# Making the low parts of 16 projection weights on VectorE instead of GpSimd, in a two-layer decoder step

## The chip, the cores and the metric

The kernel runs on one core of a Trainium2 chip. The metric is device time in microseconds for one execution of the whole program: the median of the runs shown, lower is better. A core has TensorE (PE in the profile), VectorE (DVE), ScalarE (ACT), GpSimd (POOL) and SyncE (SP), which here only issues transfers.

## The reference

One inference step of a decoder trunk with two layers, for a prompt of 1024 tokens and 8 samples of 8 tokens (1088 columns in all), with D = 1024. Cut to what matters:

```python
# layer 0
y, ... = mix_ab(hp, ...)      # y = concatenate([a_out, b_out], -1) @ w_out   (w_out 1024 x 1024)
xp = xp + y
# layer 1
yp, kp, vp = swa_prompt(...)  # y = o.reshape(N, T, N_HEADS * HEAD_DIM) @ w_o   (w_o 1024 x 1024)
ys, ks_, vs_ = swa_sample(...)
xp, xs = xp + yp, xs + ys
# each layer, after that
xp = xp + mem_attend(rmsnorm(xp, ln_mem[l]), mk, mv, m_w_q[l], m_q_gain[l], m_w_o[l])
xp = xp + conv_ffn(rmsnorm(xp, ln_ffn[l]), ...)
```

The two output projections are `@ w_out` in layer 0 and `@ w_o` in layer 1. All of it is float32.

## The kernel before

**Precision.** TensorE multiplies operands of type fp32r, and each product of the large projections is made of three: a value is split into a high part (a copy to fp32r) and a low part (the value minus its high part), and `mm3` (lines 259 to 261) adds high times high, high times low and low times high into one PSUM tile. So every weight and every activation tile needs two instructions before TensorE can use it: an ACTIVATE on ScalarE for the high part, and a subtraction for the low part. For a weight, `split_w` (lines 228 to 235) makes both for a tile of 128 partitions x 1024 elements: line 233 the high part, line 234 the low part. Line 234 runs on the engine that its argument names, `(eng or P)`, so on GpSimd if none is given. For an activation, `split_act` makes both, on ScalarE (line 360) and VectorE (line 361).

**The output projections.** `out_proj` (line 603) is called once in each layer. It goes through pairs (g, c): g is one of four groups of 256 output rows, c one of three chunks of the 1088 columns (384, 384 and 320). For a group it calls the loader twice, which gives two weights of 128 x 1024. Then, for each of eight blocks k of the inputs, it splits the activation tile (lines 360 and 361) and issues six matmuls, three for each of the two weights. After k = 7 `x_update` adds the two results into the residual stream: VectorE reads PSUM (line 313), GpSimd adds the old low part (line 314), ScalarE and VectorE split the sum again (292, 293), and ScalarE with GpSimd or VectorE sums its squares (300 to 305). The loader of layer 0 is `load_cols`, that of layer 1 is `load_wo`, inside `swa`. Each makes eight weights in a run, 16 in all.

**Around them.** In layer 0 the projection follows the values of the gating block: `v_tile` for nine tiles t (lines 539 to 547, with a step on GpSimd at 547), and `gate(t)`, four matmuls (line 559), a sum on VectorE (562 or 564) and a product on GpSimd (568). `gate(7)` and `gate(8)` stand in the middle of the projection, behind step 11. In layer 1 the attention of the samples runs in steps between those of the projection (`next(smp)`): scores, a softmax over the keys (lines 1673 to 1688, with eight exponentials on ScalarE at 1683), transposes, values (1718, 1719).

**Order and buffers.** The order on TensorE is that of the code. The order on every other engine is made by a scheduler at build time, which models the durations; each engine then runs its row strictly in that order. A load lands in one of three staging tiles `st`, which comes free when the low part has been made. The weights' parts live in ten tiles `w`, two for each weight.

Of the kernel before, what the change touches and what calls it, by code (L numbers as in the profile page):

```python
# [71 lines left out]
def kernel(  # L72
# [10 lines left out]
    V, S, P, T = nc.vector, nc.scalar, nc.gpsimd, nc.tensor  # L83
    mm = T.matmul

    def pool(name, bufs=1, **kw):
        return tc.tile_pool(name=name, bufs=bufs, reuse_waits="tile", **kw)
# [7 lines left out]
    def f(ap):  # L95
        return ap.bitcast(F32)

    def psA():
        return pa.tile([128, 512], F32, tag="a", name="psa")
# [39 lines left out]
    def stage():  # L139
        return wp.tile([128, 1024], F32, tag="st", name="st", bufs=3)  # L140
# [4 lines left out]
    def wtile():  # L145
        return Pair(wslot(), wslot())
# [81 lines left out]
    def split_w(st, shape, gain, eng=None):  # L228
        if gain is not None:
            v = st.rearrange("p (k m) -> p k m", k=shape[0])  # L230
            (eng or P).tensor_tensor(out=v, in0=v, in1=gain.unsqueeze(2).to_broadcast([128, shape[0], shape[1]]), op=ALU.mult)
        w = wtile()
        S.activation(w[:, 0, :], st, AF.Copy)
        (eng or P).tensor_tensor(out=w[:, 1, :], in0=st, in1=f(w[:, 0, :]), op=ALU.subtract)
        return w

    def load_cols(src, c0, gain=None, k=KB, eng=None):
        st = stage()
        m = 1024 // k
        nc.sync.dma_start(out=st.rearrange("p (k m) -> p k m", k=k),  # L240
                          in_=src[:, c0:c0 + m].rearrange("(k p) m -> p k m", p=128))
        w = split_w(st, (k, m), gain, eng)
        return w.rearrange("p s (k m) -> p s k m", k=k)
# [14 lines left out]
    def mm3(out, ah, al, bh, bl, first, last):  # L258
        mm(out, lhsT=ah, rhs=bh, start=first, stop=False)  # L259
        mm(out, lhsT=ah, rhs=bl, start=False, stop=False)  # L260
        mm(out, lhsT=al, rhs=bh, start=False, stop=last)  # L261
# [48 lines left out]
    def x_update(c, m, ps):  # L310
        n = CHS[c][1]
        t1 = tmp()[:, :n]
        V.tensor_tensor(out=t1, in0=ps[:, :n], in1=f(xh[c][:, m, :]), op=ALU.add)
        P.tensor_tensor(out=t1, in0=t1, in1=f(xl[c][:, m, :]), op=ALU.add)
        if c == 2:
            nc.sync.dma_start(out=xd[:, m, :], in_=t1)
        split_x(c, m, t1)
# [40 lines left out]
    def split_act(pl, src_n, src, tag="s3"):  # L358
        t = pl.tile([128, 2, 384], F32R, tag=tag, name=tag)
        S.activation(t[:, 0, :src_n], src, AF.Copy)  # L360
        V.tensor_tensor(out=t[:, 1, :src_n], in0=src, in1=f(t[:, 0, :src_n]), op=ALU.subtract)  # L361
        return t
# [48 lines left out]
    def mix0(sst):  # L411
        w_in = ab_w_in[0]
        with ExitStack() as es:
# [138 lines left out]
            def gate(t):  # L552
                c, o, w = tile_of(t)
                vt = vts.pop(t)
                ps = psB()
                pv = ps.rearrange("p (g i) -> p g i", g=4)[:, :, :w]
                for g in range(4):
                    rhs = wst[:, g, :] if t < 8 else bd[:, g, :]
                    mm(pv[:, g, :], lhsT=vt[:w, 128 * g:128 * g + 128], rhs=rhs, start=True, stop=True)
                sg = bp.tile([128, 4, 128], F32, tag="sg", name="sg", bufs=1)  # L560
                if t < 8:
                    V.tensor_tensor(out=sg, in0=pv, in1=bsb, op=ALU.add)
                else:
                    V.tensor_tensor(out=sg[:, :, :64].rearrange("p g (n t) -> p g n t", t=8),
                                    in0=pv.rearrange("p g (n t) -> p g n t", t=8),
                                    in1=bsb[:, :, 0:8].unsqueeze(2).to_broadcast([128, 4, 8, 8]), op=ALU.add)
                uv = u32[:, :, 128 * t:128 * t + w]
                P.tensor_tensor(out=uv, in0=uv, in1=sg[:, :, :w], op=ALU.mult)
# [15 lines left out]
            for t in range(NT):  # L584
# [3 lines left out]
                if t == 3:  # L588
                    pool_states()
                    e2.close()  # L590
                    sp = es.enter_context(pool("m0o", 9))
# [2 lines left out]
                if t == 5:  # L594
                    conv_ctx(0)
            src = lambda k, c: (u32 if k < 4 else b32)[:, k % 4, CHS[c][0]:CHS[c][0] + CHS[c][1]]
            for i, _ in enumerate(out_proj(src, lambda m: load_cols(ab_w_out[0], 128 * m), sp,
                                           [(g, c) for g in range(4) for c in range(3)])):
                if i == 11:
                    gate(7)  # L600
                    gate(8)

    def out_proj(src, loader, sp, order):
        ws = {}
        for g, c in order:
            if g not in ws:
                ws[g] = [loader(2 * g), loader(2 * g + 1)]
            n = CHS[c][1]
            pss = [psA(), psA()]
            for k in range(KB):  # L610
                s3 = split_act(sp, n, src(k, c))
                for i in range(2):
                    w = ws[g][i]
                    mm3(pss[i][:, :n], w[:, 0, k, :], w[:, 1, k, :], s3[:, 0, :n], s3[:, 1, :n], k == 0, k == KB - 1)
                if k == KB - 1:
                    for i in range(2):
                        x_update(c, 2 * g + i, pss[i])
                yield g, c, k
# [844 lines left out]
    def swa(wkv):  # L1463
        sc = 64.0 ** -0.5
        with ExitStack() as es:
            bp = es.enter_context(pool("swa"))
            qo = bp.tile([128, 8, 1088], F32, name="qo")
            if True:
# [260 lines left out]
                def load_wo(m):  # L1729
                    st = stage()  # L1730
                    sv = st.rearrange("p (g j m) -> p g j m", g=2, j=4)
                    src = c_w_o[0][:, 128 * m:128 * m + 128].rearrange("(g w j d) m -> w g d j m", g=2, w=2, j=4)
                    for w in range(2):
                        for g in range(2):
                            nc.sync.dma_start(out=sv[64 * w:64 * w + 64, g], in_=src[w, g])
                    wt = split_w(st, None, None)
                    return wt.rearrange("p s (k m) -> p s k m", k=KB)

                for t in range(NT):
# [32 lines left out]
                sp = es.enter_context(pool("swao", 5))  # L1772
                src = lambda k, c: qo[:, k, CHS[c][0]:CHS[c][0] + CHS[c][1]]
                order = [(0, 0), (0, 1), (1, 0), (1, 1), (0, 2), (1, 2), (2, 0), (2, 1), (2, 2), (3, 0), (3, 1), (3, 2)]
                for i, (g, c, k) in enumerate(out_proj(src, load_wo, sp, order)):
                    if i % 4 == 2:
                        next(smp, None)
                    if i == 31:
                        for _ in smp:
                            pass  # L1780

    with tc.manual_schedule(engines={mybir.EngineType.PE}):
        with ExitStack() as rs:
            with ExitStack() as es:
                open_tmp(es, 0)
                mix0(mem_kv())
                kept = mem(0, rs)
            x32, conv_out = ffn(0, *kept, rs)
            with ExitStack() as es:
                open_tmp(es, 1)  # L1790
                wkv = [load_rows(c_w_qkv[0], r, 1024, g_mix[1][:, 2 * r:2 * r + 2]) for r in range(4)]
                after_ffn(0, x32, conv_out)
                rs.close()
                swa(wkv)
                kept = mem(1, rs)
            x32, conv_out = ffn(1, *kept, rs)
            final(x32, conv_out)
# [28 lines left out]
```

## Time and profile before

| | |
|---|---|
| median of 3 runs | 2620.58 us (2615.94 to 2621.81) |
| the profiled execution, its own time | 2620.95 us |
| its span, first to last instruction | 2619.2 us |
| mean granted clock of TensorE | 0.970 |
| busy: TensorE, VectorE, ScalarE, GpSimd | 95%, 75%, 47%, 17% |

The 1.75 us between the span and the profiled execution's time lie around the program. A busy share is a mean over the whole span: VectorE is nearly always busy in some stages and half idle in others. A granted clock of 1.00 is 2.4 GHz and 0.50 is 1.2 GHz; a value between them is a mean over a stretch with both.

### The profile page before, as it was taken

The page shows a single profiled execution, that of the slowest core. Times are in us where ns is not written, and L with a number is a line of the kernel's source. Part 1 is how long each engine was busy: PE and PEld are TensorE (multiplying, and loading weights), DVE is VectorE, ACT ScalarE, POOL GpSimd, SP SyncE. Part 2 cuts the span into 40 slices and gives each one's busy share as a digit, 9 for nine tenths or more (in the row PEclk, how much of TensorE's full clock was granted, in tenths as well). Part 3 has the DMA queues.
Part 4 walks back from the last instruction along what each step waited for, and adds up shares of the span by engine and source line. Part 5 has one row for each costly group of instructions (what it writes and reads, how often), then busy time and mean ns, then how long its engine had stood idle before and what let it go on. Part 6 is the DMA issues. An engine that isn't in the chain of part 4 may idle for free.

```text
span 2619.2 us, 46210 instructions
## 1 busy us (share of the span) xinstructions
PE 2489.4 (95%) x17136; PEld 2305.6 (88%) x17136; DVE 1969.7 (75%) x4551; ACT 1232.5 (47%) x2705; POOL 456.7 (17%) x434
## 2 busy tenths in 40 slices
PE   8999999779999999999999989998699999999998
PEld 7998988679999998999876768877599999999998
DVE  7646965787878786888767676856988787777885
ACT  7324645354554544333555564553454545455331
POOL 2516532110000001110133333421100000002100
PEclk9999999889999999999999987999799999999999
DMA  8302112523333346654211011205424343348642
GB/s 278 118 12 71 64 38 93 178 83 124 116 124 124 105 129 211 220 194 141 68 39 48 1 58 49 77 26 160 140 92 135 96 130 107 120 148 294 228 143 86
DMA packets 229345, 305.53 MB, mean 117 GB/s; under 512 B 17793, under 2 KB 189919, under 8 KB 229118
## 3 DMA queue, kind: packets, MB, share of 16 engines
q1 hardware_dynamic: 213502, 227.91, 27.3%
q0 software_dynamic: 15616, 74.65, 7.9%
q8 instruction: 135, 2.21, 0.4%
q14 instruction: 92, 0.75, 0.1%
HBM read 217.79 MB, written 84.63 MB: 115 GB/s over the span
## 4 chain that ended last, share of the span: by engine, by line
issue 31%; PE 30%; DVE 11%; DMA 4%; ACT 3%; POOL 1%; SPq 0%; ACTq 0%; DVEq 0%; POOLq 0%
PE psa L1021 3%; PE psa L1022 3%; PE psa L1023 3%; PE psa L259 3%; PE psa L260 3%; PE psa L261 3%; PE psb L1021 2%; PE psb L1023 2%; PE psb L1022 2%; DMA st<-in_f_w_down_dram 2%; DVE s L361 1%; PE psb L167 1%; DVE w L1070 1%; DVE x L1393 1%; PE psa L1622 1%
## 5 line engine op out<-in xcount | busy, mean ns | idle before, releaser
L1069 ACT ACTIVATE w<-st 128x512 fp32r<-128x512 f32 (+2 forms) x532 | 299.0, 572 | 381.1 <-PE psb L1023 103.8
L1070 DVE TENSOR_TENSOR w<-st,w 128x512 fp32r<-128x512 f32 (+2 forms) x532 | 325.8, 617 | 180.4 <-ACT w L1069 171.3
L1021 PE MATMUL psa<-b,w 128*128 128x272 f32 x1152 | 334.4, 290 | 20.5 <-ACT b L1105 12.5
L1022 PE MATMUL psa<-b,w 128*128 128x272 f32 x1152 | 332.7, 289 | 9.0 <-DVE b L1106 9.0
L1023 PE MATMUL psa<-b,w 128*128 128x272 f32 x1152 | 333.3, 289 | 0.0
L1021 PE MATMUL psa<-big,w 128*128 128x272 f32 x960 | 280.7, 292 | 8.0 <-ACT x L1391 4.0
L1023 PE MATMUL psa<-big,w 128*128 128x272 f32 x960 | 280.2, 292 | 1.5 <-DVE w L1070 1.5
L1022 PE MATMUL psa<-big,w 128*128 128x272 f32 x960 | 278.9, 290 | 0.0
L1021 PE MATMUL psb<-big,w 128*128 128x272 f32 x888 | 257.4, 290 | 0.7 <-ACT x L1391 0.4
L1023 PE MATMUL psb<-big,w 128*128 128x272 f32 x888 | 257.3, 290 | 0.0
L1022 PE MATMUL psb<-big,w 128*128 128x272 f32 x888 | 256.5, 289 | 0.0
L1021 PEld LDWEIGHTS psa<-b,w 128*128 128x128 f32 x1152 | 217.4, 189 | 22.6 <-ACT b L1105 13.1
L1022 PEld LDWEIGHTS psa<-b,w 128*128 128x128 f32 x1152 | 217.3, 189 | 11.4 <-DVE b L1106 11.4
L1023 PEld LDWEIGHTS psa<-b,w 128*128 128x128 f32 x1152 | 217.2, 189 | 0.0
L260 PE MATMUL psa<-s,w 128*128 128x384 f32 (+1 forms) x576 | 199.5, 346 | 13.8 <-DVE s L361 13.5
L259 PE MATMUL psa<-s,w 128*128 128x384 f32 (+1 forms) x576 | 199.9, 347 | 2.6 <-ACT s L360 2.6
L1021 PE MATMUL psb<-b,w 128*128 128x272 f32 x696 | 201.6, 290 | 0.0
L1022 PE MATMUL psb<-b,w 128*128 128x272 f32 x696 | 200.4, 288 | 1.2 <-DVE b L1377 1.2
L1023 PE MATMUL psb<-b,w 128*128 128x272 f32 x696 | 201.5, 289 | 0.0
L261 PE MATMUL psa<-s,w 128*128 128x384 f32 (+1 forms) x576 | 196.1, 340 | 0.0
L1021 PEld LDWEIGHTS psa<-big,w 128*128 128x128 f32 x960 | 182.8, 190 | 10.7 <-DVE x L1393 5.8
L1023 PEld LDWEIGHTS psa<-big,w 128*128 128x128 f32 x960 | 183.5, 191 | 1.9 <-DVE w L1070 1.9
(367 smaller groups left out, 6585.1 us busy)
## 6 DMA issues: line engine op xcount, KB each, us to landing
st<-in_f_w_up_dram SPq DMA_DIRECT2D x88, 512.0 KB
hd<-big SPq DMA_DIRECT2D x264, 136.0 KB
hd<-m SPq DMA_DIRECT2D x176, 136.0 KB
big<-hd POOLq DMA_DIRECT2D x48, 408.0 KB, 7.2
st<-in_f_w_down_dram SPq DMA_DIRECT2D x48, 384.0 KB
b<-hd POOLq DMA_DIRECT2D x18, 816.0 KB, 7.3
big<-hd POOLq DMA_DIRECT2D x18, 816.0 KB, 7.7
ks<-in_m_w_kv_dram SPq DMA_DIRECT2D x16, 512.0 KB
```

The source lines that it names most:

```text
L167: T.transpose(out, in_, idt[:rows, :rows])
L259: mm(out, lhsT=ah, rhs=bh, start=first, stop=False)
L260: mm(out, lhsT=ah, rhs=bl, start=False, stop=False)
L261: mm(out, lhsT=al, rhs=bh, start=False, stop=last)
L361: V.tensor_tensor(out=t[:, 1, :src_n], in0=src, in1=f(t[:, 0, :src_n]), op=ALU.subtract)
L1021: mm(ps[:, :QT], lhsT=wt[:, 0, k, :], rhs=bt[:, 0, k, :], start=first and k == 0, stop=False, skip_group_check=True)
L1022: mm(ps[:, :QT], lhsT=wt[:, 0, k, :], rhs=bt[:, 1, k, :], start=False, stop=False, skip_group_check=True)
L1023: mm(ps[:, :QT], lhsT=wt[:, 1, k, :], rhs=bt[:, 0, k, :], start=False, stop=k == nk_of(j) - 1, skip_group_check=True)
L1069: S.activation(t[:, 0], src, AF.Copy)
L1070: V.tensor_tensor(out=t[:, 1], in0=src, in1=f(t[:, 0]), op=ALU.subtract)
L1393: V.tensor_tensor(out=x, in0=ps, in1=x, op=ALU.add)
L1622: mm(po[64 * two:64 * two + 64, :], lhsT=vv[:, t + 1 - nb + kb, 64 * (2 * g + two):64 * (2 * g + two) + 64], rhs=pTs[two, kb], start=(kb = ...
```

## The change

Both loaders now hand VectorE to `split_w`, so that line 234 runs on VectorE for the 16 weights of the two output projections. The other 16 instructions of line 234 stay on GpSimd.

```diff
@@ mix0
-            for i, _ in enumerate(out_proj(src, lambda m: load_cols(ab_w_out[0], 128 * m), sp,
+            for i, _ in enumerate(out_proj(src, lambda m: load_cols(ab_w_out[0], 128 * m, eng=V), sp,
                                            [(g, c) for g in range(4) for c in range(3)])):
@@ swa, load_wo
-                    wt = split_w(st, None, None)
+                    wt = split_w(st, None, None, V)
```

What follows is how the build places them. TensorE's row is the same before and after.

On VectorE, in layer 0 around the last two tiles of the gating block. `vt_2123` is tile 7 and `bn_2170` belongs to tile 8; `s3_2292` and `s3_2301` are the first two activation tiles of the chunk (g = 0, c = 1); the `w` tiles are the low parts of weights 2 to 5. The signs are those of the difference, after against before:

```order
 L335 TENSOR_SCALAR s_2130<-mv_2127 128x1
+L234 TENSOR_TENSOR w_2198<-st_2195,w_2197 128x1024
 L546 TENSOR_SCALAR vt_2123<-vt_2123,mv_2127,s_2129 128x512
+L234 TENSOR_TENSOR w_2489<-st_2486,w_2488 128x1024
 L361 TENSOR_TENSOR s3_2292<-u32_742,s3_2292 128x384
+L234 TENSOR_TENSOR w_2495<-st_2492,w_2494 128x1024
 L541 BN_STATS bn_2170<-vt_2168 64x6
 L562 TENSOR_TENSOR sg_2186<-psb_2181,bsb_746 128x512
+L234 TENSOR_TENSOR w_2773<-st_2770,w_2772 128x1024
 L543 BN_AGGR mv_2172<-bn_2170 64x2
-L335 TENSOR_SCALAR s_2175<-mv_2172 64x1
 L361 TENSOR_TENSOR s3_2301<-u32_742,s3_2301 128x384
```

Four low parts now stand ahead of the last steps of tile 8, and of the tiles of chunk 1.

On VectorE, in layer 1, early in the projection. `s3_17285`, `s3_17294` and `s3_17303` are the activation tiles k = 0, 1 and 2 of (g = 0, c = 1), the next ones that TensorE needs there; 1678 to 1688 are the softmax of the samples; `psa_17174` and `psa_17175` are the results of (0, 0):

```order
 L361 TENSOR_TENSOR s3_17259<-qo_14310,s3_17259 128x384
+L361 TENSOR_TENSOR s3_17285<-qo_14310,s3_17285 128x384
 L1678 TENSOR_TENSOR s_17207<-s_17205,snks_91 128x8
+L361 TENSOR_TENSOR s3_17294<-qo_14310,s3_17294 128x384
+L313 TENSOR_TENSOR t_17268<-psa_17174,big_72 128x384
+L313 TENSOR_TENSOR t_17275<-psa_17175,big_72 128x384
 L1684 TENSOR_TENSOR s_17210<-s_17210,s_17207 128x8
 L1686 RECIPROCAL s_17220<-s_17210 128x8
-L313 TENSOR_TENSOR t_17268<-psa_17174,big_72 128x384
+L361 TENSOR_TENSOR s3_17303<-qo_14310,s3_17303 128x384
 L1688 TENSOR_TENSOR k4_17080<-k4_17080,s_17220 128x1088
-L361 TENSOR_TENSOR s3_17285<-qo_14310,s3_17285 128x384
```

The three activation tiles, which stood behind 1684 to 1688, now stand ahead of 1688, two of them ahead of 1684. ScalarE's row moves with them: the high parts of the first two now stand ahead of the eight exponentials instead of behind.

On VectorE, in layer 1, where the third group begins. `s3_17814` and `s3_17823` are activation tiles of (1, 2), and the two `w` tiles are weights 6 and 7:

```order
 L313 TENSOR_TENSOR t_17767<-psa_17686,big_72 128x320
+L234 TENSOR_TENSOR w_17883<-st_17877,w_17882 128x1024
 L361 TENSOR_TENSOR s3_17814<-qo_14310,s3_17814 128x320
+L234 TENSOR_TENSOR w_18164<-st_18158,w_18163 128x1024
 L361 TENSOR_TENSOR s3_17823<-qo_14310,s3_17823 128x320
 L293 TENSOR_TENSOR big_72<-t_17759,big_72 128x320
```

Two low parts now stand between activation tiles of the chunk in work.

## Rows read from the trace of the kernel before

**Rows 1.** The page: busy time, share of the span and instructions of each engine.

```profile
PE 2489.4 (95%) x17136; PEld 2305.6 (88%) x17136; DVE 1969.7 (75%) x4551; ACT 1232.5 (47%) x2705; POOL 456.7 (17%) x434
```

**Rows 2.** Waits of TensorE: who for whom, us in total, times, longest.

```profile
PE psa L260 <- DVE s L361: 13.5, 15, 2.5
...
PE psb L352 <- DVE rvq L305: 8.6, 2, 4.4
```

**Rows 3.** Stretches: length, busy PE, PEld, DVE, ACT, POOL; PE clock, DMA, GB/s.

```profile
244.40:255.00 10.60, 8.20 (x39) 7.51 (x39) 5.48 (x11) 4.43 (x12) 7.67 (x8) 0.84 0.06 15
255.00:292.00 37.00, 36.68 (x224) 35.95 (x223) 36.76 (x57) 25.64 (x57) 18.97 (x14) 1.00 0.11 38
292.00:301.00 9.00, 7.07 (x32) 6.75 (x32) 9.00 (x12) 4.90 (x13) 5.54 (x4) 0.82 0.48 143
...
1553.90:1564.10 10.20, 6.76 (x21) 5.63 (x20) 9.72 (x14) 6.17 (x15) 6.21 (x4) 0.67 0.20 52
...
1622.00:1632.40 10.40, 7.27 (x28) 6.75 (x28) 10.19 (x13) 5.69 (x11) 7.70 (x6) 0.67 0.43 133
```

**Rows 4.** Groups of GpSimd: busy us, mean ns of one, idle before.

```profile
L234 POOL TENSOR_TENSOR w<-st,w 128x1024 fp32r<-128x1024 f32 x32 | 82.1, 2572 | 54.4 <-ACT w L233 53.2 <-DMA st<-in_ab_w_in_dram 1.2
```

**Rows 5.** Groups of VectorE, shapes apart; columns as in the group before.

```profile
L361 DVE TENSOR_TENSOR s<-b,s 128x384 fp32r<-128x384 f32 x32 | 16.9, 560 | 0.0
...
L1597 DVE TENSOR_TENSOR k<-k,s 128x1024 f32<-128x1024 f32 x14 | 17.1, 1225 | 0.2
```

**Rows 6.** GpSimd in order of time: start us, us, idle before and its releaser.

```profile
227.71 4.94 POOL L234 TENSOR_TENSOR w<-st,w 128x1024 fp32r<-128x1024 f32 x2
...
264.46 2.72 POOL L234 TENSOR_TENSOR w<-st,w 128x1024 fp32r<-128x1024 f32 x1
...
1431.36 2.37 POOL L234 TENSOR_TENSOR w<-st,w 128x1024 fp32r<-128x1024 f32 x1 [7.09 <-ACT w L233]
```

**Rows 7.** VectorE in order of time; columns as in the group before.

```profile
227.78 2.62 DVE L546 TENSOR_SCALAR vt<-vt,mv,s 128x512 f32<-128x512 f32 x1 [1.65 <-POOL s L336]
...
234.44 7.28 DVE L361 TENSOR_TENSOR s<-u,s 128x384 fp32r<-128x384 f32 x3
...
264.84 3.90 DVE L361 TENSOR_TENSOR s<-u,s 128x384 fp32r<-128x384 f32 x2
...
293.27 3.76 DVE L255 SCALAR_TENSOR_TENSOR w<-st,vec,w 128x512 fp32r<-128x512 f32 x2
...
1428.28 0.15 DVE L1594 TENSOR_TENSOR s<-s 128x4 f32<-128x4 f32 x1
...
1431.41 2.34 DVE L1594 TENSOR_TENSOR s<-s 128x4 f32<-128x4 f32 x1 [1.51 <-ACT s L1593]
...
1521.86 2.35 DVE L1594 TENSOR_TENSOR s<-s 128x4 f32<-128x4 f32 x1
...
1554.35 0.17 DVE L1684 TENSOR_TENSOR s<-s 128x8 f32<-128x8 f32 x1 [2.87 <-ACT k L1683]
...
1555.09 1.28 DVE L1688 TENSOR_TENSOR k<-k,s 128x1088 f32<-128x1088 f32 x1
```

**Rows 8.** TensorE in order of time; columns as in group 6.

```profile
245.69 1.16 PE L559 MATMUL psb<-bd,vt 64*128 64x64 f32 x8 [1.26 <-POOL vt L547]
...
297.55 0.50 PE L260 MATMUL psa<-s,w 128*128 128x384 f32 x1 [1.93 <-DVE s L361]
...
1436.05 1.09 PE L167 MATMUL psa<-idt,k 128*128 128x128 f32 x8 [2.84 <-POOL k L1597]
...
1557.70 0.69 PE L260 MATMUL psa<-s,w 128*128 128x384 f32 x1 [2.48 <-DVE s L361]
...
1564.03 1.97 PE L167 MATMUL psb<-idt,k 128*128 128x128 f32 x16
...
1626.55 0.64 PE L260 MATMUL psa<-s,w 128*128 128x320 f32 x1 [2.48 <-DVE s L361]
```

**Rows 9.** ScalarE in order of time, layer 0, the fifth weight.

```profile
233.84 1.06 ACT L233 ACTIVATE w<-st 128x1024 fp32r<-128x1024 f32 x1 [1.18 <-DMA st<-in_ab_w_out_dram]
```

## The prediction, made before the changed kernel ran

> **What bounds the kernel now.** I began with the page's engine line: TensorE is busy 95% of the span, GpSimd 17% [rows 1]. So the end is set by TensorE's work and by the few places where it waits or runs at a lower clock; a change off TensorE can win or lose only there. Next I read TensorE's waits, for places that the change can reach. It waits 13.5 us in 15 waits for the activation low parts of line 361, which VectorE makes in the row in which the new work is put, and 8.6 us for rvq of line 305 [rows 2], behind a projection. Then the stretches of the two projections, engine by engine [rows 3]. Read the VectorE column first: 36.76 of 37 us, 9.00 of 9. Where the projection runs, VectorE is full although its mean is 75%. From 255 to 292 TensorE keeps pace all the same (36.68, clock 1.00). In the four other stretches it doesn't:
>
> - 244.4 to 255: idle 10.60 − 8.20 = 2.40, clock 0.84
> - 292 to 301: idle 1.93, clock 0.82
> - 1553.9 to 1564.1: idle 3.44, clock 0.67
> - 1622 to 1632.4: idle 3.13, clock 0.67
>
> A clock under 1.00 is time on the 1.2 GHz level, and the rows show it behind each of these idles. Its cost is at most (1 − clock) times the length: 1.7, 1.6, 3.4 and 3.4 us. Some of that is idle counted again, so I take three quarters of it.
>
> **The price of one line 234.** On GpSimd it is 2.57 us, 32 times [rows 4]. On VectorE there is no such row. The nearest is line 1597, the same shape with two inputs from SBUF: 1.225 us [rows 5]. So VectorE gets 16 x 1.23 = 19.6 us of work. At first sight that is bad, since it is the full engine.
>
> But look at what VectorE does while GpSimd runs line 234. At 1431.41 it starts line 1594, 128 x 4 elements, which took 0.15 us three us before; now 2.34. It ends with GpSimd's instruction, which ran from 1431.36 to 1433.73 [rows 6, 7]. At 227.78, under two of line 234, a line 546 takes 2.62 us; from 234.44 three of line 361 take 7.28 together and from 264.84 two take 3.90 [rows 7], where one is 0.56 [rows 5]. So in these places VectorE already pays about 2.2 us for a low part that GpSimd makes. Making it itself costs 1.23 and takes the 2.2 away: a gain of about 1.0 us of VectorE, not a loss. What may hide here is the reverse: next to GpSimd's remaining line 314 a line 234 on VectorE may be stretched too. I bound it by 1.23 (as line 1597) and 2.57 (as on GpSimd) and take 1.23, since GpSimd loses its longest instruction in these stages.
>
> **Where it reaches TensorE.** Six places, in time.
>
> *244.4 to 255.* TensorE waits 1.26 us at 245.69 for GpSimd's line 547 of tile 8 [rows 8]. That waited for line 546 on VectorE, behind the stretched tiles of [rows 7]. The new row has four low parts ahead of that tile, 4 x 1.23 = 4.9 us; the four instructions that leave GpSimd there blocked VectorE for about 4 x 2.2 = 8.8. So tile 8 comes about 4 us sooner and the wait, the low clock behind it and the later short waits go: 2.40 + 0.75 x 1.7 = 3.7 us. One condition: the fifth weight's high part ran only at 233.84, after a wait for its load [rows 9], since its staging tile came free only with an earlier low part. VectorE's row now stops at that low part if the load is late. As the low parts before it are made sooner, the load is issued sooner on SP's queue, so I cost this at nothing; uncovered, it would cost about the 1.2 us of that wait.
>
> *292 to 301.* One low part on GpSimd stretches two of line 255 to 3.76 us in all [rows 7] and TensorE waits 1.93 for line 361 at 297.55 [rows 8]. With 1.0 us less in the row and a shorter head of it, I take idle and clock: 1.93 + 0.75 x 1.6 = 3.1.
>
> *1431.* TensorE waits 2.84 at 1436.05 for line 1597 on GpSimd [rows 8], whose softmax sum was line 1594, stretched to 2.34. One low part now stands in that row instead: 2.34 − 1.23 = 1.1.
>
> *1521.* The same stretched line 1594, 2.35 [rows 7], and no wait of TensorE that I can tie to it alone: 0.5.
>
> *1553.9 to 1564.1.* Here the order itself changes. Before, VectorE stood 2.87 us idle at line 1684 for the exponentials and then did line 1688, 1.28 us [rows 7], with the next activation tiles behind both; TensorE waited 2.48 at 1557.70 [rows 8]. In the 10.2 us before its transposes at 1564.03 it does only 21 matmuls [rows 3], which at full clock are 3.4 us (36.68 for 224 in the stretch from 255). In the new row these tiles stand ahead of 1688 and two ahead of 1684, so TensorE works through the exponentials. I leave 1.3 us of waits, chosen, since the transposes need the softmax and the exponentials now stand behind two more high parts on ScalarE: 10.2 − 3.4 − 1.3 = 5.5.
>
> *1622 to 1632.4.* TensorE waits 2.48 at 1626.55 for line 361 [rows 8]. Two low parts now stand among the tiles of that chunk, 2 x 1.23, so most of the wait is only exchanged for another. Of 3.13 + 0.75 x 3.4 = 5.7 I take 2.0.
>
> Sum: 3.7 + 3.1 + 1.1 + 0.5 + 5.5 + 2.0 = 15.9. Against the profiled execution, 2620.95, 0.4 over the median: **2605**. The other low parts (227 to 243, 255 to 292, 1538 to 1557) lie where TensorE keeps pace; there the exchange costs nothing as long as VectorE's row gets shorter. GpSimd's line 314, 547 and 568 no longer queue behind 2.6 us, which I count as nothing since VectorE, not GpSimd, is last there. The wait for rvq behind the projections can move either way by the order of a few 0.4-us steps: ±1.5, in the range.
>
> **Rivals.**
> *Only the order counts.* If VectorE needs 2.57 for line 234 beside GpSimd's other work, each exchange is 2.2 for 2.57, and nothing is left but the 5.5 of the fourth stretch: 2615.5. For it: 314 and 305 still run beside it. Against: the sixteen include many with GpSimd otherwise idle.
> *No change.* The waits are given back later: at the edge to the memory attention, where TensorE waits up to 4.4 us for rvq [rows 2], or at the exponentials. About 2621. Against: VectorE's last work before that edge is shortened too.
> *Slower, a full VectorE.* If VectorE loses under a line 234 of GpSimd less than 1.23 us, the exchange is a loss. That is its deciding point. Twelve of the 16 start in a stretch of [rows 3] or under a stretched row of [rows 7] (the other four at 216, 1539, 1548 and 1620); if GpSimd had cost it nothing there, the price would be 12 x 1.23 = 14.8 us: 2636. With half of that hidden, 2628. Against it are the 2.34, 7.28 and 3.90 of [rows 7], all over that point.
> A rule speaks here: the Trainium skill, "Perfetto Trace Analysis", Optimizing Scalar/DVE Operations, says that a saturated VectorE is a reason to hand work to GpSimd, but that the two share a port to SBUF, so that handing over may not help. By its first half this change goes the wrong way and ends near 2636; by its second half GpSimd's share was not free. The stretched rows of VectorE in this trace side with the second half.
>
> **The numbers.** The forecast has a chance of 0.70, order only 0.12, no change 0.10, slower 0.08. The forecast's own range is 2597 to 2613: the lower end is all idle and the whole bound on the clock of the four stretches (10.9 + 10.1 = 21.0) plus the 2.84 at 1436, 23.8 in all; the upper is half of the sum. What a measurement of this kernel can tell from no change is about 0.2%, 5.2 us. Faster by more: 0.70 and half of "order only", 0.76; within: the other half and "no change", 0.16; slower: 0.08. The range for 8 in 10 is 2596 to 2617, with the forecast and "order only", and with 1.5 for rvq.
>
> **What would show it.** In the profile after: line 234 of VectorE 16 times at a mean near 1.23, and of GpSimd 16 times; near 2.5 on VectorE the first rival holds. Line 1594 in layer 1 at 0.15 each time. No wait for line 547 near 245, TensorE's clock 1.00 through the stretches that answer to the first two, the group of transposes after (0, c = 1)'s third block some 5.5 us sooner against the start of that chunk, and the waits for line 361 well under 13.5. The prediction is wrong if VectorE stops at low parts whose load or high part is late, if the wait for line 361 grows, or if the 16 us are gained by the end of each projection and lost again at the rvq wait behind it.

## The result, and the profile after

| | before | after |
|---|---|---|
| median | 2620.99 us (2615.94 to 2621.81, 4 runs) | 2605.55 us (2601.87 to 2606.19, 4 runs) |
| ratio to before | | 0.9946, 95% interval 0.9934 to 0.9958 |
| span of the profiled run | 2619.2 us | 2604.4 us |
| mean granted clock | 0.970 | 0.973 |

The median before is that of the three runs given ahead and one more. The change makes the kernel 15.4 us faster, and the time is about half a us from the forecast of 2605.

The page after, to be read beside [rows 1]:

```profile
PE 2480.4 (95%) x17136; PEld 2297.3 (88%) x17136; DVE 1958.7 (75%) x4567; ACT 1232.0 (47%) x2705; POOL 421.8 (16%) x418
```

VectorE has 16 instructions more and is busy 11.0 us less. The groups of line 234 after, with one of line 361, as in [rows 4, 5] (busy us, mean ns of one, idle before):

```profile
L234 POOL TENSOR_TENSOR w<-st,w 128x1024 fp32r<-128x1024 f32 x16 | 40.5, 2543 | 33.3 <-ACT w L233 18.2 <-PE psb L167 15.1
...
L361 DVE TENSOR_TENSOR s<-u,s 128x384 fp32r<-128x384 f32 x32 | 23.4, 759 | 0.0
L234 DVE TENSOR_TENSOR w<-st,w 128x1024 fp32r<-128x1024 f32 x16 | 22.1, 1383 | 2.9 <-ACT w L233 2.9
```

So 22.1 us were added and 1969.7 − 1958.7 + 22.1 = 33.1 us went away: on average 2.07 us of VectorE for each low part that left GpSimd, against 1.38 for making it there. A third of it went from that one group of line 361, which before was:

```profile
L361 DVE TENSOR_TENSOR s<-u,s 128x384 fp32r<-128x384 f32 x32 | 34.7, 1113 | 0.0
```

The waits of TensorE after, as in [rows 2]:

```profile
PE psa L260 <- DVE s L361: 9.6, 16, 1.1
...
PE psb L352 <- DVE rvq L305: 5.7, 2, 4.7
```

The wait for line 361 has lost 3.9 us and its longest pieces (2.5 to 1.1). For the stretches, the windows below hold the same work as those of [rows 3]; the second answers to 255 to 292 (columns: length, busy PE, PEld, DVE, ACT, POOL; PE clock, DMA, GB/s):

```profile
246.00:253.00 7.00, 6.66 (x39) 5.93 (x38) 2.79 (x6) 2.65 (x7) 3.67 (x4) 1.00 0.02 4
253.00:289.40 36.40, 36.40 (x225) 36.20 (x224) 35.40 (x60) 26.65 (x59) 16.36 (x13) 1.00 0.13 38
289.40:296.10 6.70, 5.83 (x32) 5.24 (x31) 6.70 (x10) 4.87 (x12) 2.38 (x3) 1.00 0.54 193
1548.40:1552.50 4.10, 3.61 (x20) 2.98 (x19) 3.97 (x7) 4.10 (x12) 1.99 (x2) 1.00 0.49 159
1612.00:1616.90 4.90, 4.22 (x27) 4.22 (x28) 4.90 (x11) 2.94 (x6) 0.99 (x2) 1.00 0.60 209
```

The clock is 1.00 in all five. In the last four VectorE is nearly as full as before, yet TensorE waits far less. The last window opens inside a wait and leaves out another one just ahead of it, so that place is measured over a longer stretch further down. Its row in order of time at the places of [rows 8]:

```profile
246.11 1.10 PE L559 MATMUL psb<-bd,vt 64*128 64x64 f32 x8
...
293.83 0.45 PE L260 MATMUL psa<-s,w 128*128 128x384 f32 x1 [0.86 <-DVE s L361]
...
1432.83 1.09 PE L167 MATMUL psa<-idt,k 128*128 128x128 f32 x8 [1.69 <-POOL k L1597]
...
1552.52 1.94 PE L167 MATMUL psb<-idt,k 128*128 128x128 f32 x16 [0.15 <-DVE k L1688]
...
1612.68 0.42 PE L260 MATMUL psa<-s,w 128*128 128x320 f32 x1 [1.06 <-DVE s L361]
```

The wait of 1.26 for line 547 is gone, 1.93 has become 0.86, 2.84 has become 1.69. VectorE at two of these places, as in [rows 7]:

```profile
1430.35 0.15 DVE L1594 TENSOR_TENSOR s<-s 128x4 f32<-128x4 f32 x1
...
1549.96 1.22 DVE L361 TENSOR_TENSOR s<-qo,s 128x384 fp32r<-128x384 f32 x1
1551.10 1.28 DVE L1688 TENSOR_TENSOR k<-k,s 128x1088 f32<-128x1088 f32 x1
```

Line 1594 is back at 0.15 (none of its 32 takes more than 0.17), and the third activation tile runs ahead of 1688.

### The profile page after: what moved, and what is told of

It is laid out like the page before. It is cut to its first block, busy times and chain, and to the rows that moved or that the text cites. A ratio compares the mean times of both kernels' runs of the same rounds, so it can differ in the third digit from the quotient of the medians.

```text
span 2604.4 us, 46204 instructions
## 1 busy us (share of the span) xinstructions
PE 2480.4 (95%) x17136; PEld 2297.3 (88%) x17136; DVE 1958.7 (75%) x4567; ACT 1232.0 (47%) x2705; POOL 421.8 (16%) x418
## 5 line engine op out<-in xcount | busy, mean ns | idle before, releaser
L260 PE MATMUL psa<-s,w 128*128 128x384 f32 (+1 forms) x576 | 196.0, 340 | 10.0 <-DVE s L361 9.6
L259 PE MATMUL psa<-s,w 128*128 128x384 f32 (+1 forms) x576 | 195.5, 339 | 2.4 <-ACT s L360 2.4
L1021 PEld LDWEIGHTS psa<-big,w 128*128 128x128 f32 x960 | 182.9, 191 | 11.1 <-DVE x L1393 5.1
L261 PE MATMUL psa<-s,w 128*128 128x384 f32 (+1 forms) x576 | 192.1, 333 | 0.0
```

The source lines that it names most:

```text
L1021: mm(ps[:, :QT], lhsT=wt[:, 0, k, :], rhs=bt[:, 0, k, :], start=first and k == 0, stop=False, skip_group_check=True)
```

## The experiments

The theory ("exchange"): a low part on GpSimd holds VectorE for about 2.2 us, on VectorE it costs 1.4, TensorE gains where it waits for VectorE, and the new order in layer 1 adds its own part. The rivals: only the order counts; a full VectorE pays for every us that it is given; and, since the mean clock rose, that more than half of the gain is granted clock which fell elsewhere by chance.

**Half the change: layer 0 alone, layer 1 alone.**

```diff
-out_proj(src, lambda m: load_cols(ab_w_out[0], 128 * m), ...
+out_proj(src, lambda m: load_cols(ab_w_out[0], 128 * m, eng=V), ...
```

> Only the eight low parts of layer 0 on VectorE; layer 1 as before. Theory 'exchange' (a low part on GpSimd holds VectorE for about 2.2 us, on VectorE it costs about 1.4, and TensorE gains where it waited for VectorE): the two places of layer 0 gain 4.0 and 2.7 us and 1.3 are given back behind them, so 5.4 in all, about 2615.6 us, and the stretches of layer 1 keep their idle. Rival 'order only' (the exchange is worth nothing, only the new place of the activation tiles in layer 1 counts): about 2621. Rival 'clock' (more than half of the 15 us are granted clock that falls elsewhere by chance): a time anywhere between the two kernels, with the stretches of layer 0 no better than before.

Measured: 2614.61 us, ratio 0.9980 (0.9971 to 0.9990).

```diff
-wt = split_w(st, None, None)
+wt = split_w(st, None, None, V)
```

> Only the eight low parts of layer 1 on VectorE; layer 0 as before. 'Exchange' with the order: 1.5 at the first weight, 0.5 at the second, 5.3 at the chunk (0, 1), 3.6 at the third group, 10.9 in all, about 2610 us. 'Order only': 5.5, about 2615.5. 'Clock': anything between 2605 and 2621.

Measured: 2610.15 us, ratio 0.9962 (0.9949 to 0.9974), beside 2620.21 for the kernel before. The gains, 5.6 and 10.1, add up to 15.7; the whole change has 15.4. "Order only" gave layer 0 nothing, so it falls. Both halves came out within 1 us of "exchange", which "clock" has no reason for.

**The order: one weight alone, and all but that one.** It is the low part of the fourth weight of layer 1 whose move sets the two activation tiles of (0, 1) ahead of 1684.

```diff
-wt = split_w(st, None, None)
+wt = split_w(st, None, None, V if m in (3,) else P)
```

> One low part alone, that of the fourth weight of layer 1, on VectorE; 31 stay on GpSimd. In the rows of this kernel the first two activation tiles of (0, 1) stand ahead of 1684 as in the changed kernel. Both 'exchange' and 'order only' give the chunk (0, 1) its 5 us by the order alone, about 2616 us; the idles of 244 to 255, 292 to 301 and of the third group stay. If the gain at that chunk is the low part leaving GpSimd and not the order, the next kernel has most of it and this one little.

Measured: 2620.40 us, ratio 1.0003 (0.9995 to 1.0012). No gain: the expectation missed.

```diff
-wt = split_w(st, None, None, V)
+wt = split_w(st, None, None, V if m in (0, 1, 2, 4, 5, 6, 7) else P)
```

> All low parts of both projections on VectorE but that of the fourth weight of layer 1. The activation tiles of (0, 1) then stand behind 1688 as in the kernel before. 'Exchange': all gains but the 5 us of that chunk, about 2610 to 2611 us, and in that chunk a wait of over 2 us for line 361 stays. 'Order only': about 2621.

Measured: 2611.57 us, ratio 0.9968 (0.9958 to 0.9977); TensorE waits 2.47 us for line 361 in that chunk. This kernel keeps the old order there and still gains 8.6 us over the kernel before, where "order only" said about 2621, so that rival falls here too. And with the fifteen others in place the fourth weight is worth 6.0 us (2611.57 − 2605.55), and alone nothing. The trace of the run with that weight alone shows why. TensorE:

```profile
1562.80 0.69 PE L260 MATMUL psa<-s,w 128*128 128x384 f32 x1 [3.72 <-DVE s L361]
```

VectorE of the same run, with the third tile as the first of the four:

```profile
1558.30 1.83 DVE L1688 TENSOR_TENSOR k<-k,s 128x1088 f32<-128x1088 f32 x1
1560.05 4.91 DVE L361 TENSOR_TENSOR s<-qo,s 128x384 fp32r<-128x384 f32 x4
```

And GpSimd, with the low part of the fifth weight:

```profile
1558.93 3.40 POOL L234 TENSOR_TENSOR w<-st,w 128x1024 fp32r<-128x1024 f32 x1
```

TensorE passes the first two tiles and stops at the third. That one stands behind 1688 in this kernel's row and ends with GpSimd's low part.

A second stop stands in the same trace, near the end of the chunk before, (0, 0). TensorE, VectorE and ScalarE there:

```profile
1552.04 0.45 PE L260 MATMUL psa<-s,w 128*128 128x384 f32 x1 [2.07 <-DVE s L361]
...
1549.09 1.23 DVE L234 TENSOR_TENSOR w<-st,w 128x1024 fp32r<-128x1024 f32 x1 [2.83 <-ACT w L233]
...
1548.00 1.06 ACT L233 ACTIVATE w<-st 128x1024 fp32r<-128x1024 f32 x1 [3.94 <-DMA st<-in_c_w_o_dram]
```

VectorE stood 2.83 us at the fourth weight's low part, whose load was late, with the activation tiles behind it; after the whole change it stood 0.36 us at the same low part. So this run pays for two things that the whole change does not have: the late load, and the hold at the third tile.

For the third tile, two kernels part the two causes: one takes GpSimd's low part away and leaves the tile behind 1688, the other the reverse.

```diff
-wt = split_w(st, None, None)
+wt = split_w(st, None, None, V if m in (3, 4) else P)
```

> The fourth and the fifth weight of layer 1 on VectorE, the other 30 on GpSimd. The third activation tile of (0, 1) still stands behind 1688 in the row, as with the fourth weight alone, but no low part of GpSimd runs beside it. If the 3.72 us wait of the run with the fourth weight alone came from GpSimd holding VectorE (1688 took 1.83 for 1.28, and the tile ended with GpSimd's low part), the wait falls by about 2.3 to 1.4 us, and the time to about 2617. If it came from the place behind 1688 alone, the wait stays over 3 and the time at 2620.

Measured: 2614.40 us, ratio 0.9982 (0.9973 to 0.9992), and TensorE at the third tile:

```profile
1559.55 0.44 PE L260 MATMUL psa<-s,w 128*128 128x384 f32 x1 [1.46 <-DVE s L361]
```

```diff
-wt = split_w(st, None, None)
+wt = split_w(st, None, None, V if m in (0, 1, 2, 3) else P)
```

> The first four weights of layer 1 on VectorE. All three activation tiles of (0, 1) stand ahead of 1688, as in the changed kernel, and the low part of the fifth weight is on GpSimd. If the place of the third tile decides, the chunk gains its 5 us and the first two weights 2.0: about 2613.5 us. If GpSimd's fifth low part decides, a wait of 2 to 3 us for line 361 stays in the chunk, one block later, and the time is about 2617.

Measured: 2612.74 us, ratio 0.9973 (0.9963 to 0.9982), beside 2619.49 for the kernel before. The waits in and around that chunk are 0.15, 0.37 and 0.44 us. Of the 3.72 us about 2.3 came from the hold, as expected, and the rest from the place behind 1688. Both kernels gain, 5.1 and 6.8 us, the second with the first weights' share. The first still has the late load (VectorE stands 2.55 us, TensorE 2.07), so against the run with the fourth weight alone it shows what the hold cost: 4.1 us on TensorE's row from 1546 to 1570, and 5.3 by the gains over the kernel before. No run takes away the late load alone; what it cost is not shown.

**The price: each low part made twice.**

```diff
         (eng or P).tensor_tensor(out=w[:, 1, :], in0=st, in1=f(w[:, 0, :]), op=ALU.subtract)
+        if twice or (eng is V and shape is not None):
+            V.tensor_tensor(out=w[:, 1, :], in0=st, in1=f(w[:, 0, :]), op=ALU.subtract)
```

(`twice` is set in `load_wo`.)

> The changed kernel with each of the 16 low parts made twice on VectorE, the same values into the same tile. 'Exchange' says that the price then is 2 x 1.38 = 2.8 us against the 2.2 that VectorE lost before: where it is full, each costs 1.4 more, about five of them in TensorE's path, and some clock behind it: 7 to 10 us slower than the changed kernel, 2612 to 2616, so better than before by the order alone. If VectorE had slack, the time stays at 2605.5; if VectorE were the bound at all sixteen, 22 us are lost and it ends near 2627.

Measured: 2621.81 us, ratio 1.0010 (1.0000 to 1.0019). The whole gain is gone, the order's part too; expected were 2612 to 2616. The second copies are the first of these groups:

```profile
L236 DVE TENSOR_TENSOR w<-st,w 128x1024 fp32r<-128x1024 f32 x16 | 22.5, 1409 | 0.1
L234 DVE TENSOR_TENSOR w<-st,w 128x1024 fp32r<-128x1024 f32 x16 | 21.7, 1358 | 4.3 <-ACT w L233 4.3
```

16.3 us for 22.5 us of VectorE, 0.7 for one: VectorE is indeed near the bound at most of the sixteen. On TensorE's row the largest piece, 6.7 us, is in layer 1 around the chunk (0, 1), where the softmax comes later; the next, 4.6 us, is in layer 0. TensorE at both (line numbers are two higher in this kernel, 1690, 561 and 549 are 1688, 559 and 547):

```profile
1560.24 3.65 PE L167 MATMUL psb<-idt,k 128*128 128x128 f32 x16 [3.80 <-DVE k L1690]
...
250.90 1.45 PE L561 MATMUL psb<-bd,vt 64*128 64x64 f32 x8 [4.10 <-POOL vt L549]
```

And GpSimd ahead of the latter, with a line 568 that stands before tile 8's steps in its row, and tile 8's line 547:

```profile
238.04 5.69 POOL L570 TENSOR_TENSOR u<-u,sg 128x512 f32<-128x512 f32 x1 [5.15 <-DVE sg L564]
...
249.27 1.58 POOL L549 TENSOR_TENSOR vt<-vt,vgb 64x512 f32<-64x512 f32 x1
```

GpSimd's product takes 5.69 us where eight of them took 1.35 on average before: here it is VectorE that holds GpSimd, and tile 8 comes later than before. By a straight line between 1.38 us a low part (2605.5) and 2 x 1.38 (2621.8) the change would win nothing at about 2.6 us.

**The hold: GpSimd's low parts in four pieces.**

```diff
-        (eng or P).tensor_tensor(out=w[:, 1, :], in0=st, in1=f(w[:, 0, :]), op=ALU.subtract)
+        for q in range(4 if eng is None else 1):
+            qs = slice(256 * q, 256 * q + 256) if eng is None else slice(0, 1024)
+            (eng or P).tensor_tensor(out=w[:, 1, qs], in0=st[:, qs], in1=f(w[:, 0, qs]), op=ALU.subtract)
```

> The kernel before, with each of GpSimd's low parts (those whose loader names no engine) made in four pieces of 256 columns. If GpSimd holds VectorE for a whole instruction of its own, line 1594 of layer 1 takes 0.8 us at most in place of 2.34, and about 1.5 us are won at the first weight; elsewhere VectorE is full, and meets a piece at each of its own instructions: no more than 2 us in all, 2619 to 2622. If the two engines only share a rate, line 1594 still takes 2.3.

Measured: 2619.31 us, ratio 0.9994 (0.9982 to 1.0007). Line 1594 (1596 here) under the first weight of layer 1, which started at 1431.65 on GpSimd:

```profile
1431.70 0.69 DVE L1596 TENSOR_TENSOR s<-s 128x4 f32<-128x4 f32 x1 [1.85 <-ACT s L1595]
```

0.69 in place of 2.34: about one piece. So VectorE doesn't run slower, it stands until GpSimd's instruction ends. The Trainium skill, "SBUF — State Buffer", Who interferes with whom, says the same: a VectorE instruction with two inputs in SBUF and a GpSimd instruction that reads SBUF shut each other out for a whole instruction, whichever began first. The trace agrees in both directions (2.34 and 0.69 on VectorE, 5.69 on GpSimd). Smaller pieces gain nothing in time. The expectation's reason, that a full VectorE meets the next piece, fits, but no run tests it apart.

**Further in the same direction.** Line 314 of `x_update`, on the changed kernel and on the one before:

```diff
-        P.tensor_tensor(out=t1, in0=t1, in1=f(xl[c][:, m, :]), op=ALU.add)
+        V.tensor_tensor(out=t1, in0=t1, in1=f(xl[c][:, m, :]), op=ALU.add)
```

> The changed kernel with line 314, too, on VectorE: 48 instructions in the x_update of the projections, 1.22 us each on GpSimd, about 0.55 on VectorE by line 313 of the same shape. 'Exchange': if each held VectorE for about 1.0 us it now costs 0.55, and where VectorE is full TensorE gains some of the difference: 3 to 6 us better than the changed kernel, 2600 to 2603. Rival: line 314 did not hold VectorE for that long; then 48 x 0.55 = 26 us are added to a full engine, and at 0.7 us of time for each us of VectorE (the doubled low parts: 16.3 us for 22.5) that is 18 us slower, near 2623.

Measured: 2587.14 us, ratio 0.9893 (0.9876 to 0.9910), the lowest median of the study.

> The kernel before with line 314 on VectorE; all low parts of weights on GpSimd. If the gain of line 314 does not depend on where the low parts are made, it is the same 3 to 6 us: 2615 to 2618. If line 314 only matters where low parts queue it on GpSimd, this one gains more than the one on the changed kernel.

Measured: 2604.56 us, ratio 0.9948 (0.9931 to 0.9965), beside 2618.39 for the kernel before. Both moved the expected way and three to four times as far (18.4 and 13.8 us against 3 to 6). The page of the former, with its group:

```profile
PE 2470.2 (96%) x17136; PEld 2294.4 (89%) x17136; DVE 1951.6 (75%) x4615; ACT 1233.9 (48%) x2705; POOL 372.1 (14%) x370
...
L314 DVE TENSOR_TENSOR t<-t,big 128x384 f32<-128x384 f32 x32 | 17.4, 549 | 0.0
...
L314 DVE TENSOR_TENSOR t<-t,big 128x320 f32<-128x320 f32 x16 | 12.1, 756 | 0.1
```

VectorE got 29.5 us and its busy time fell by 7.1 against the changed kernel: 36.6 us of holds went, 0.76 each, for 0.61. That is the exchange again, but 7.1 us of VectorE at 0.7 are 5 us, not 18. Part of the 18 is not the edit's. The kernel before was at 2618.39 beside these runs and at 2620.99 beside the changed kernel, so by the gains over it the difference is 15.8. In the two traces, TensorE's work of the projections (before: 240 to 365 and 1535 to 1745) takes 317.7 us in the changed kernel and 306.6 in this one, 11.1 less; the other 7.3 lie in stretches without a line 314. A shorter way from PSUM to the split of the sum, with no change of engine in it, may be the rest of the 11; no run parts the two, and it stays open.

The softmax product of layer 1 on VectorE:

```diff
-                        E = P if two else V
+                        E = V
```

> The changed kernel with all of line 1597 (the softmax's product in layer 1) on VectorE: 16 more of 1.23 us there, 2.45 us each on GpSimd before. VectorE is not full in that stage, and TensorE waits 2.5 us in two waits for line 1597 of GpSimd. 'Exchange': those waits go and little is added, 0 to 3 us better, 2602 to 2606. Rival: two products one behind the other on VectorE come later than two side by side: 0.7 x 16 x 1.23 = 14 us slower at most.

Measured: 2612.10 us, ratio 0.9975 (0.9966 to 0.9984), 6.5 us slower than the changed kernel. The expectation missed. On TensorE's row the stretch that answers to 1420 to 1445 before is 6.0 us longer than in the changed kernel, so the loss lies there. VectorE at the first weight of layer 1:

```profile
1428.58 1.23 DVE L234 TENSOR_TENSOR w<-st,w 128x1024 fp32r<-128x1024 f32 x1 [4.12 <-ACT w L233]
```

ScalarE ahead of it, and TensorE behind it, in the same run:

```profile
1427.49 1.06 ACT L233 ACTIVATE w<-st 128x1024 fp32r<-128x1024 f32 x1 [8.84 <-DMA st<-in_c_w_o_dram]
...
1431.05 0.69 PE L167 MATMUL psb<-idt,gq 64*128 64x64 f32 x4 [7.69 <-DVE gq L1506]
```

In this kernel's row the low part stands ahead of the steps 1503 to 1506, its load is late, and all of VectorE stops 4.12 us for it. That is the head-of-line wait which the prediction named in layer 0 as its condition; there it did not come, here it did.

All 32 low parts on VectorE, with line 314 there too (the edits of line 314, and `eng=V` at the three other `load_cols`, which also moves the eight multiplications of line 231):

> The kernel with line 314 on VectorE and all 32 low parts (with the gains of line 231) on VectorE. The first eight lie where the loads set the pace, the last eight in the memory attention, where GpSimd has time and VectorE is 60% busy: 0 to 2 us better than with line 314 alone by 'exchange', as the holds go there too; if the holds only count where VectorE is full, the same time.

Measured: 2587.72 us, ratio 0.9890 (0.9875 to 0.9904): no different from line 314 alone. The other 16 low parts don't stand where VectorE is full, and moving them wins nothing.

## Why the prediction was right, step by step

Each place is measured on TensorE's row between the same two matmuls, before and after.

| place | predicted | measured |
|---|---|---|
| 244 to 255 | 3.7 | 3.7 (11.71 to 8.05) |
| 292 to 301 | 3.1 | 2.3 (8.89 to 6.60) |
| 1431 | 1.1 | 1.2 (5.91 to 4.74) |
| 1521 | 0.5 | 0.0 |
| 1554 to 1564 | 5.5 | 5.2 (9.25 to 4.07) |
| 1622 to 1632, taken from 1621 to 1640 | 2.0 | 2.7 (19.01 to 16.27) |

The sum of these is 15.1 against 15.9, and the span fell by 14.8. The step on the price held: 1.38 us on VectorE near the bound of 1.23, 2.07 freed where 2.2 was read from the stretched rows. So did the step on tile 8, "about 4 us sooner": line 546 of tile 8 starts at 240.90 after 243.05 while TensorE is 1.75 us later in its work there, 3.9 us together:

```profile
243.05 0.53 DVE L546 TENSOR_SCALAR vt<-vt,mv,s 64x512 f32<-64x512 f32 x1
...
240.90 0.54 DVE L546 TENSOR_SCALAR vt<-vt,mv,s 64x512 f32<-64x512 f32 x1 [1.69 <-POOL s L336]
```

The second line, after the change, also shows what the prediction counted as nothing because "VectorE, not GpSimd, is last there": now VectorE waited 1.69 us for GpSimd's line 336, which stood behind the stretched line 568 of the last section. It cost TensorE no wait. The condition that the prediction put on the fifth weight held as well: its high part waited 1.18 us for its load after the change too, and VectorE did not stop there. It stopped at four other low parts for their high parts, 2.9 us in all, 1.36 of them at the first weight of layer 1, where the place gained its 1.2 all the same.

The order step gave its 5.2 us, but its reason was half told. The prediction put it all on the tiles that stand ahead; the runs with single weights show that the two tiles ahead alone win nothing, as TensorE stops at the third if GpSimd's fifth low part holds VectorE there, and ahead of it if the fourth weight's load is late. The 5.2 is also one trace against one: with layer 0 alone changed, and so nothing here, this stretch takes 6.3 us and not 9.25. From 1546 to 1570 the two traces without the change have 24.1 and 22.4 us, the changed kernel and the one with layer 1 alone 18.8 and 18.5, so the place is worth 3.6 to 5.5 us.

The term of 1622 to 1632 came out near its size and for its reason, that a wait is mostly exchanged for another. The windows below hold the same 78 matmuls before and after (columns as in [rows 3]), then come the waits in them:

```profile
1621.09:1640.10 19.01, 15.88 (x78) 15.11 (x77) 18.80 (x23) 11.40 (x24) 12.20 (x8) 0.82 0.41 133
...
1609.46:1625.73 16.27, 13.67 (x78) 12.41 (x77) 16.27 (x26) 10.86 (x24) 6.83 (x5) 1.00 0.51 164
...
1622.92 0.42 PE L260 MATMUL psa<-s,w 128*128 128x320 f32 x1 [0.65 <-DVE s L361]
...
1610.47 0.42 PE L260 MATMUL psa<-s,w 128*128 128x320 f32 x1 [0.70 <-DVE s L361]
...
1621.65 0.45 PE L260 MATMUL psa<-s,w 128*128 128x384 f32 x1 [0.83 <-DVE s L361]
```

Before, TensorE waited 0.65 and 2.48 us and ran on at the low clock; after, it waits 0.70, 1.06 and 0.83 at a clock of 1.00. Counted only up to 1632 and from behind the new waits the place would seem to gain 5.4, but the waits ahead and behind give half of it back. The runs with layer 0 alone and with the first four weights, which leave this place as it was, need the same 19.0 us for it, and the one with layer 1 alone 16.3, so here the gain is the change's. VectorE is full throughout (18.80 of 19.01, 16.27 of 16.27): TensorE gained about what VectorE had less to do, 0.9 us for each of the three low parts there, where the prediction priced 1.0.

Outside these places gains and losses nearly cancel. One stretch early in the run, and one ahead of layer 1's attention, after the change:

```profile
48.00:54.00 6.00, 4.90 (x18) 3.97 (x19) 4.51 (x8) 5.40 (x10) 0.00 (x0) 0.72 1.03 349
...
1287.00:1293.00 6.00, 6.00 (x32) 5.18 (x32) 2.81 (x11) 1.84 (x5) 1.52 (x2) 0.52 0.60 212
```

Before, the clock was 1.00 in both; by TensorE's row these places lost 2.6 and 4.0 us, while from 1525 to 1545 it won 3.1 with a higher clock and from 347 to 357 another 1.6. The first lies ahead of every changed instruction. Such shifts of 2 to 4 us are as large as the spread of single runs, and that the forecast was hit to 0.5 us is in part luck; that the halves add up in medians to 15.7 does not.

Of the rivals, "only the order counts" fell with layer 0 alone and with the fourth weight left out. The slower end, a full VectorE, had the right deciding point: at twice the price the gain is gone, and the crossing near 2.6 us is not far from the 2.07 that a low part held VectorE.

## What to carry to other kernels

A full engine can become less full by taking work over, if the neighbour that did the work held it for longer than the work takes: look for tiny instructions that last as long as the neighbour's, and end with it, and compare that hold with the price of the same shape on the full engine. Then find each place where TensorE waits for that engine, and cost the change there alone; low parts elsewhere won nothing. Check what stands behind a moved instruction in its new row: one late load stops all of it.

## What the runs showed of the hardware

VectorE's instructions, one close behind the other, can hold GpSimd over several of them. After the change one of GpSimd's products of line 568 took 4.14 us; its usual time is 1.3:

```profile
236.22 4.14 POOL L568 TENSOR_TENSOR u<-u,sg 128x512 f32<-128x512 f32 x1 [2.88 <-DVE sg L562]
```

From 236.00 to 239.21 VectorE ran a low part and four tiles of line 361 almost without a gap, and the product ended 1.15 us after the last of them, about its own time. So GpSimd did not get in between. It isn't so every time. Before the change, VectorE had this tile just ahead of the two from 264.84 [rows 7]:

```profile
264.08 0.83 DVE L361 TENSOR_TENSOR s<-b,s 128x384 fp32r<-128x384 f32 x1
```

GpSimd's low part from 264.46 [rows 6] ran in between, and the two took 3.90 us. What decides is not shown. Cut in four, a low part took 4 x 0.88 = 3.5 us of GpSimd for 2.57 whole.
